# One-hot rows of the expert weights: two tokens taking turns in memory instead of four

## The chip, the cores and the metric

The kernel runs on one core of one Trainium2 chip. The metric is the device time of one execution in microseconds; the median of 3 runs of the kernel before is 2192.8 us (2192.29 to 2193.07). All arithmetic is in the kernel.

## The reference

The program is a model of two blocks over 256 tokens with 1024 features: two layers of attention of three kinds between feed-forwards, then a block with two recurrent mixers (mLSTM and gated linear attention, with a context of 256 tokens), and at its end a layer of 16384 small experts (128 x 128 of them), whose part matters here:

- Eight heads give every token scores against 128 first and 128 second keys; the 16 best of a head's sums name 16 experts by (first index, second index), with a softmax over the 16 as weights. So a token has 8 x 16 = 128 pairs.
- An expert is a row u and a row v of 1024 numbers. The output is the sum over a token's 128 pairs of weight x gelu(x . u[expert]) x v[expert]. Here gelu is the activation function.

## The kernel before, in words

Features or pairs lie on the 128 partitions, tokens along the free dimension. All large products take each operand in two float32 parts (`mm3`, lines 256 to 258: three matmuls of 128 x 128 stationary by 256 moving columns). Weights come by DMA in pieces of 128 x 1024, and are split into their two parts by ScalarE (line 218, `wH`) and VectorE (line 219, `wL`); each of these has three buffers.

The expert layer (`peer`) does not gather experts. It computes the activation of all 16384 experts for all tokens into A [128, 128 tiles, 256 tokens] (`u_chunk`, two tiles each, 64 chunks), multiplies A by a matrix G that holds a token's weight where one of its pairs falls and 0 elsewhere, and then takes the product with all rows v (`v_chunk`, 64 chunks). The first 32 chunks of u run while pairs are chosen. The other 32 run between the steps that make G: 16 groups of 16 tokens, a group being four calls of `g_unit` (four tokens each) and two chunks.

`g_unit` makes G for four tokens. The 128 pairs of a token lie on the partitions. In a tile `o` of f16 it makes, for each pair, the row of 128 that is 1 at the second index (part 0), the row that is 1 at the first index (part 1), and the latter times the pair's weight in two parts (2 and 3):

- line 1268, VectorE: compares a table of indices `i4` with the tokens' indices `ix`; parts 0 and 1, 1024 elements per partition.
- line 1270, VectorE: part 2 = part 1 x the weights' high part `wH` (512 elements).
- line 1272, ScalarE: part 3 = part 1 x the weights' low part `wL`, one copy of 128 elements per token.
- line 1275, TensorE: for each token two matmuls in f16 add up part 2 or 3 (stationary) times part 0 (moving) over the 128 pairs: a tile of G, 128 first by 128 second indices, in PSUM.
- lines 1278 and 1280: VectorE multiplies the first n1 tiles of A by it, ScalarE stores the rest for later. n1 grows from 64 to 124 over the groups.

In `o` the four tokens are the innermost dimension: element i of a row is followed by element i of the next token's row. So a row that a matmul reads has its elements four apart, 8 bytes; the same goes for ScalarE's copies. `o` has two buffers, PSUM's bank `at` four. The order on each engine is laid down when the program is built; in the trace, all but the first matmuls of line 1275 stand in runs of 16, two calls of `g_unit`, with the 48 matmuls of half a group's chunks (one chunk) between two runs.

Of the kernel before, what the change touches and what calls it, by code (L numbers as in the profile page):

```python
# [29 lines left out]

def tiles_of(w, cols):
    """[K, N] -> [128, len(cols), K/128, 128]: column tiles as stationary operands; -1 pads with 0."""
    w = np.asarray(w)
    kt = w.shape[0] // 128
    w = np.concatenate([w, np.zeros((w.shape[0], 1), w.dtype)], axis=1).reshape(kt, 128, -1)
    return w[:, :, np.asarray(cols)].transpose(1, 2, 0, 3)
# [6 lines left out]
def rows_of(w):  # L43
    """[K, N] -> [128, K/128, N]."""
    w = np.asarray(w)
    return w.reshape(-1, 128, w.shape[1]).transpose(1, 0, 2)


def col_of(v):
    """[..., n*128] -> [128, n]: a vector over features, one column per tile."""  # L50
    return np.asarray(v).reshape(-1, 128).T
# [96 lines left out]
def gate_rows(mg, glr):  # L148
    """Rows of the tile of gates: quadrants ig d0 + glr d0, ig d1 + glr d1, f d0, f d1."""
    g = [-1] * 128  # L150
    for d in range(2):
        for h in range(4):
            g[32 * d + h] = mg + 8 * d + h
            g[64 + 32 * d + h] = mg + 8 * d + 4 + h
        if glr is not None:
            for r in range(16):
                g[32 * d + 16 + r] = glr + 16 * d + r
    return g
# [46 lines left out]
class W:  # L205
    """Weights [128, cols] of DRAM in two float32r parts, in pieces of cut columns."""
# [22 lines left out]
class Halves:  # L229
    """A [128, KT, T] array in two tiles, indexed [:, k] or [:, a:b] within one of them."""  # L230
# [11 lines left out]
class K:  # L242
# [5 lines left out]
    # -- streams of weights --------------------------------------------------------------------  # L248
# [3 lines left out]
    def mm3(self, out, w, c, x, k, first, last, skip=False):  # L252
        """out += W[:, c:c+128]^T x[k], each operand in two parts."""
# [6 lines left out]
    def mm3t(self, out, x, k, t, w, c, n, first, last, pick=lambda v: v):  # L260
        """out[tok, n] += x[k][:, tok tile t]^T W[c:c+n]."""
# [10 lines left out]
    # -- norms -----------------------------------------------------------------------------------  # L272
# [14 lines left out]
    def stats_many(self, items):  # L287
        """For each x [128, kt, T]: 1 / rms, over all partitions [128, T], and per token [128, 2]."""
# [17 lines left out]
        out = []  # L306
# [12 lines left out]
    def sums(self, x, g=None, sq=None):  # L319
        """Sums of the squares of x [128, KT, T] (times g[k]) over the features: PSUM [128 tokens, 2].  # L320
        sq [128, KT, T]: where the squares go, otherwise to tiles of their own."""
# [21 lines left out]
    def spread(self, r, tag, pool):  # L343
        """r [128 tokens, 2] -> [128, T], the same on every partition."""
# [8 lines left out]
    def split_scaled(self, x, g, kt, tag="x"):  # L353
        """The two parts of x[k] * g[k]."""
# [16 lines left out]
    def hold(self, t):  # L371
        """The load of t that follows waits for the tile of the feed-forward that is under way: weights come first."""
        if self.mark is not None:
            self.nc.gpsimd.tensor_copy(t[:, :1], self.mark[:, :1])
# [8 lines left out]
    # -- feed-forward ----------------------------------------------------------------------------  # L383
    def ffn(self, name, l, side=iter(()), every=1, down=1):
        """side: steps of something else, taken between tiles."""
# [34 lines left out]
    # -- attentions ------------------------------------------------------------------------------  # L420
    def rope(self, dst, src, n, tab, rows=slice(0, 128), split=None):
        """dst = rope(src); src, dst [rows, n, T]; halves of a head lie in one tile."""
# [17 lines left out]
    def head(self, q, k, bias, scale, v, o):  # L440
        """One head: q, k [rows, T] features first; bias [128, 384]; v(kt) [128 keys, 64]; o PSUM [64, T]."""
# [28 lines left out]
    def mixer(self, l):  # L470
# [17 lines left out]
        # indexer  # L488
# [30 lines left out]
        # scores of the indexer  # L519
# [42 lines left out]
        # queries and keys of C  # L562
# [28 lines left out]
        # top 64 of each row: eight at a time are taken out  # L591
# [12 lines left out]
        def attend(h, q, k, bias, scale, v):  # L604
            """Head h of the 16; its half of a tile of features, which is split when both halves are there."""
# [39 lines left out]
        # output: the tiles of B and C first, then those of A  # L645
# [14 lines left out]
    # ==== second block =========================================================================  # L660
    def modulation(self, pool):
        """Steps that make mod[:, j, 0/1]: tile j of the 6 D values for the latents / the context."""
# [21 lines left out]
    def first_norm(self):  # L684
        """x of the first block, and its modulated norm in two parts."""
# [11 lines left out]
        # the second norm's mean square is that of x * gain times r1^2  # L697
# [12 lines left out]
    def modnorm(self, x, g, sc, sh, tag="x"):  # L710
        """rmsnorm(x) * g * (1 + sc) + sh in two parts."""
# [8 lines left out]
    def split_mod(self, x, a, rb, sh, tag="x"):  # L720
        """The two parts of x[k] * a[k] * rb + sh[k]."""
# [20 lines left out]
    def conv(self, dst, p, j, rows):  # L742
        """dst [128, T] = conv(p), p in PSUM, channels of tile j."""
# [8 lines left out]
    def values(self, n, xs, dst):  # L752
        """dst(t) [128 tokens, 512]: values, tokens on partitions, in steps."""
# [12 lines left out]
    def projections(self, xs, lat, gk, gq, mk, mq, mv):  # L766
        """All projections but the gates, in steps; mk, mq before their silu."""
# [8 lines left out]
        def keys(c, lo, n):  # L776
            """Tiles lo.. of src[c]; the first ones may be gq[1]."""
# [22 lines left out]
    def side(self, xs, lat):  # L800
        """Projections of one side, and what the states of both mixers need of it, in steps."""
# [5 lines left out]
        # gates, rows 32 d + h; logarithms of the sigmoids of the gates and of the decay of the GLA  # L807
# [20 lines left out]
        # tiles that the states of the mLSTM need lie outside of the pool: those of the context are made late  # L828
# [9 lines left out]
        # running sums and maxima of the mLSTM  # L838
# [17 lines left out]
        # the running maximum: m[j], M[j] = max(m[j], ce[j]), m[j+1] = be[j] + M[j]  # L856
# [17 lines left out]
        # sums of the decay of the GLA  # L874
# [10 lines left out]
        # exponentials of the mLSTM  # L885
# [5 lines left out]
        # a[j] = exp(m[j] - M[j]) on every partition  # L891
# [24 lines left out]
        # per token columns  # L916
# [6 lines left out]
        # exponentials of the GLA  # L923
# [17 lines left out]
        if lat:  # L941
# [4 lines left out]
            # weights of the pairs of tokens of the mLSTM, before the products of queries and keys  # L946
# [20 lines left out]
        # states of the GLA  # L967
# [47 lines left out]
        # keys of the mLSTM, tokens on partitions  # L1015
# [7 lines left out]
        # states of the mLSTM: C[:, h, d] = [e, (d, n)]  # L1023
# [20 lines left out]
    def gates(self, xs, gr, mo):  # L1044
        """Output gates, in steps: tiles 0-3 of the GLA, tiles 4-7 of the mLSTM; tile i lies in src[6 + (i + 1) // 2]."""
# [12 lines left out]
    def norm_heads(self, h, dst, g, gate):  # L1058
        """dst(t-major h [128, 2, 4, 128]) -> parts of gate * g * h / rms(h), features first."""
# [22 lines left out]
    def mlstm_out(self, s, gates):  # L1082
# [26 lines left out]
        # 1 / max(|den|, exp(-m))  # L1109
# [51 lines left out]
    def top16(self, z, vals, idx, n):  # L1161
        """The 16 largest of each row of z [128, n], in order, and where they stand; z is used up."""
# [8 lines left out]
    def peer(self):  # L1171
# [5 lines left out]
        with ExitStack() as es:  # L1177
            op = es.enter_context(tc.tile_pool(name="po", bufs=1))
            # activations of the experts, tile j: those of second index j; its end is scratch at first
            A = op.tile([128, 128, T], F32, name="A")  # L1180
            # per pair of a token, four tokens at a time: second indices, first indices; weights times 2^14 in two parts
# [3 lines left out]
            i4 = op.tile([128, 128, 4], F16, name="i4")  # L1185
            nc.vector.tensor_copy(i4, iota[:, :, None].to_broadcast([128, 128, 4]))
# [3 lines left out]
            def u_chunk(c, g=None):  # L1190
                """Two tiles of experts. While G is made for the tokens of group g, what falls on them waits in y,
                which is returned with its place; before (None) all of it is kept, after (4) all of it is weighted."""
# [22 lines left out]
            with tc.tile_pool(name="route", bufs=1) as kp:  # L1215
# [27 lines left out]
                # softmax over the chosen  # L1243
# [19 lines left out]
            def g_unit(u, n1):  # L1263
                """The weights of the experts for four tokens: times what the first n1 tiles hold, stored for the rest."""
                q = self.bank("at")
                o = op2.tile([128, 4, 128, 4], F16, name="o", tag="tmp", bufs=2)
                t = slice(4 * u, 4 * u + 4)
                v.tensor_tensor(o[:, :2], i4[:, None].to_broadcast([128, 2, 128, 4]),  # L1268
                                ix[:, u, :, None, :].to_broadcast([128, 2, 128, 4]), op=OP.is_equal)
                v.tensor_tensor(o[:, 2], o[:, 1], wH[:, None, t].to_broadcast([128, 128, 4]), op=OP.mult)  # L1270
                for i in range(4):
                    nc.scalar.activation(o[:, 3, :, i], o[:, 1, :, i], AF.Copy, scale=wL[:, 4 * u + i:4 * u + i + 1])  # L1272
                for i in range(4):
                    for n in range(2):
                        nc.tensor.matmul(q[:, 128 * i:128 * i + 128], o[:, 2 + n, :, i], o[:, 0, :, i],  # L1275
                                         start=n == 0, stop=n == 1)
# [41 lines left out]
            # x comes back to where the weights were  # L1318
# [16 lines left out]
    def choose(self, kp, s, best, ij, rank):  # L1335
        """s [128, 2, 128]: scores by both halves -> the 16 best pairs: their sums, ij [128, 2, 16]: both indices.
        rank [128, 16, 16]: the second dimension's index."""
# [9 lines left out]
        # a pair of ranks (r1, r2) has (r1 + 1) (r2 + 1) - 1 pairs before it, none smaller: all 16 of r2 for the first  # L1347
        # r1 and 8 for each of the others are enough
# [24 lines left out]
    def context(self):  # L1373
        """What the second block takes from the context, in steps."""
# [149 lines left out]
```

## Time and profile before

| | |
|---|---|
| median of 3 runs | 2192.8 us (2192.29 to 2193.07) |
| profiled execution, first to last instruction (span) | 2190.6 us |
| TensorE busy | 2130.0 us, 97% |
| VectorE busy | 1583.2 us, 72% |
| ScalarE busy | 1172.2 us, 54% |
| mean granted TensorE clock | 0.991 of full speed |

The profile holds one execution. Its time is known as the span alone, from the first instruction to the last; what lies around the span isn't recorded, and the median stands 2.2 us above it. PE is TensorE, PEld its loads of stationary operands, DVE VectorE, ACT ScalarE, SP the queue that issues DMAs. A record of a matmul lasts until its result is out, so records overlap, and the distance between two starts tells what one costs. In rows in order of time, like instructions that follow one another stand as one row with their count, and idle time ahead of a row stands behind it in brackets, with what ended it.

### The profile page before, as it was taken

To read this page: it belongs to the slowest core of one execution; us is meant where nothing else is said; L and a number is where in the kernel's file an instruction comes from. 1 tells how busy PE (TensorE), PEld (TensorE's weight loads), DVE (VectorE), ACT (ScalarE), POOL (GpSimd) and SP (SyncE) were. 2 spreads that over 40 slices of the span, in tenths; PEclk is the share of its full clock that TensorE was granted. 3 is DMA by queue.
4 is the path that set the end of the run, shared out by engine and by line. 5 is a ranking of instruction groups with operands and counts; after the bars stand their busy time and mean duration, and the time that the engine had idled before them with its cause. 6 is when DMAs were issued, how large, how long until landed. Compare 5 with 4: busy or idle time off the path is not lost. (4 is left out here: it accounts for less than half of the span.)

```text
span 2190.6 us, 43018 instructions
## 1 busy us (share of the span) xinstructions
PE 2130.0 (97%) x17204; PEld 2050.1 (94%) x17204; DVE 1583.2 (72%) x3195; ACT 1172.2 (54%) x2003; POOL 8.0 (0%) x15
## 2 busy tenths in 40 slices
PE   8999999999999999998998998999999999999998
PEld 8999879998999997998997888999999999999997
DVE  6766967786787796777658768888877775555555
ACT  5544465444444445556446545454687775444444
POOL 0000000000000000000000000000000000000000
PEclk9999999999999999999999999999999999999999
DMA  6666435666787752454563434555544445555553
GB/s 225 220 201 188 149 96 172 205 214 227 251 271 238 224 161 87 156 190 163 160 201 112 142 99 159 182 187 182 168 136 143 141 138 180 190 188 188 190 187 125
DMA packets 115112, 385.35 MB, mean 176 GB/s; under 512 B 12768, under 2 KB 13920, under 8 KB 114784
## 3 DMA queue, kind: packets, MB, share of 16 engines
q1 hardware_dynamic: 114912, 382.61, 54.1%
q8 instruction: 135, 2.21, 0.4%
q14 instruction: 65, 0.53, 0.1%
HBM read 380.46 MB, written 2.10 MB: 175 GB/s over the span
## 5 line engine op out<-in xcount | busy, mean ns | idle before, releaser
L219 DVE TENSOR_TENSOR wL<-raw,wH 128x1024 fp32r<-128x1024 f32 (+3 forms) x716 | 812.4, 1138 | 352.0 <-ACT wH L218 349.6
L218 ACT ACTIVATE wH<-raw 128x1024 fp32r<-128x1024 f32 (+3 forms) x716 | 707.9, 992 | 635.4 <-PE mm L257 443.8
L256 PE MATMUL mm<-xH,wH 128*128 128x256 f32 x2952 | 839.8, 285 | 11.1 <-ACT xH L360 7.2
L258 PE MATMUL mm<-xH,wL 128*128 128x256 f32 x2952 | 836.4, 284 | 9.2 <-DVE wL L219 9.0
L257 PE MATMUL mm<-xL,wH 128*128 128x256 f32 x2952 | 835.6, 283 | 0.7 <-DVE xL L1080 0.4
L256 PEld LDWEIGHTS mm<-xH,wH 128*128 128x128 f32 x2952 | 560.4, 190 | 15.8 <-ACT xH L360 7.5
L258 PEld LDWEIGHTS mm<-xH,wL 128*128 128x128 f32 x2952 | 559.9, 190 | 15.5 <-DVE wL L219 12.1
L257 PEld LDWEIGHTS mm<-xL,wH 128*128 128x128 f32 x2952 | 560.0, 190 | 4.1 <-issue 1.7
L257 PE MATMUL mm<-hl,wH 128*128 128x256 f32 x1024 | 285.8, 279 | 0.0
L256 PE MATMUL mm<-hl,wH 128*128 128x256 f32 x1024 | 285.8, 279 | 0.0
L258 PE MATMUL mm<-hl,wL 128*128 128x256 f32 x1024 | 285.8, 279 | 0.0
L258 PE MATMUL mm<-hH,wL 128*128 128x256 f32 x704 | 197.7, 281 | 8.9 <-DVE wL L219 8.8
L256 PE MATMUL mm<-hH,wH 128*128 128x256 f32 x704 | 196.3, 279 | 0.0
L257 PE MATMUL mm<-hL,wH 128*128 128x256 f32 x704 | 196.3, 279 | 0.0
L256 PEld LDWEIGHTS mm<-hl,wH 128*128 128x128 f32 x1024 | 192.4, 188 | 0.0
L257 PEld LDWEIGHTS mm<-hl,wH 128*128 128x128 f32 x1024 | 192.4, 188 | 0.0
L258 PEld LDWEIGHTS mm<-hl,wL 128*128 128x128 f32 x1024 | 192.4, 188 | 0.0
L258 PEld LDWEIGHTS mm<-hH,wL 128*128 128x128 f32 x704 | 132.1, 188 | 11.7 <-DVE wL L219 11.7
L676 DVE SCALAR_TENSOR_TENSOR prod<-raw,cv 128x1024 f32<-128x1024 f32 x64 | 78.3, 1224 | 75.8 <-DMA raw<-wmod 75.0
L256 PEld LDWEIGHTS mm<-hH,wH 128*128 128x128 f32 x704 | 132.1, 188 | 0.0
L257 PEld LDWEIGHTS mm<-hL,wH 128*128 128x128 f32 x704 | 132.0, 188 | 0.0
L1272 ACT ACTIVATE o<-o,gL 128x128 f16<-128x128 f16 x256 | 96.2, 569 | 13.3 <-DVE o L1268 10.4
(451 smaller groups left out, 2514.4 us busy)
## 6 DMA issues: line engine op xcount, KB each, us to landing
raw<-ffn_gu SPq DMA_DIRECT2D x174, 512.0 KB, 4.7
raw<-ut SPq DMA_DIRECT2D x128, 512.0 KB, 3.9
raw<-vt SPq DMA_DIRECT2D x128, 512.0 KB, 3.8
raw<-win SPq DMA_DIRECT2D x58, 512.0 KB, 4.4
raw<-wmod SPq DMA_DIRECT2D x48, 512.0 KB, 4.6
raw<-ffn_d SPq DMA_DIRECT2D x64, 384.0 KB, 3.2
raw<-ffn_d SPq DMA_DIRECT2D x64, 320.0 KB, 3.4
raw<-wout SPq DMA_DIRECT2D x24, 512.0 KB, 3.7
```

What stands on the lines that cost most here:

```text
L218: k.nc.scalar.activation(H[:, :n], raw[:, :n], AF.Copy)
L219: k.nc.vector.tensor_tensor(L[:, :n], raw[:, :n], H[:, :n].bitcast(F32), op=OP.subtract)
L256: mm(out, H, xH[:, k], start=first, stop=False, skip_group_check=skip)
L257: mm(out, H, xL[:, k], start=False, stop=False, skip_group_check=skip)
L258: mm(out, L, xH[:, k], start=False, stop=last, skip_group_check=skip)
L676: nc.vector.scalar_tensor_tensor(out, raw, 1.0, cv[:, D * i:D * i + D], op0=OP.mult, op1=OP.mult, accum_out=self.mod[:, j, i:i + 1])
L1272: nc.scalar.activation(o[:, 3, :, i], o[:, 1, :, i], AF.Copy, scale=wL[:, 4 * u + i:4 * u + i + 1])
```

## The change

Tokens take turns in pairs. `o` becomes [parts, 2 pairs of tokens, 128, 2 tokens], so that a row's elements lie two apart, 4 bytes. The table of indices has two copies of each index instead of four (`i2`, 256 elements instead of 512). The comparison and the weighting still take 1024 and 512 elements in one instruction each; their repeated operand (`ix`, `wH`) is now read in runs of two tokens, each repeated 128 times, instead of runs of four. The copies and the matmuls have the same counts and sizes. The rest of the edit takes out comments, which moves lines: 1268, 1270, 1272 and 1275 become 1269, 1272, 1275 and 1279.

```diff
-            i4 = op.tile([128, 128, 4], F16, name="i4")
-            nc.vector.tensor_copy(i4, iota[:, :, None].to_broadcast([128, 128, 4]))
+            i2 = op.tile([128, 128, 2], F16, name="i2")
+            nc.vector.tensor_copy(i2, iota[:, :, None].to_broadcast([128, 128, 2]))
...
             def g_unit(u, n1):
                 q = self.bank("at")
-                o = op2.tile([128, 4, 128, 4], F16, name="o", tag="tmp", bufs=2)
+                o = op2.tile([128, 4, 2, 128, 2], F16, name="o", tag="tmp", bufs=2)
                 t = slice(4 * u, 4 * u + 4)
-                v.tensor_tensor(o[:, :2], i4[:, None].to_broadcast([128, 2, 128, 4]),
-                                ix[:, u, :, None, :].to_broadcast([128, 2, 128, 4]), op=OP.is_equal)
-                v.tensor_tensor(o[:, 2], o[:, 1], wH[:, None, t].to_broadcast([128, 128, 4]), op=OP.mult)
+                v.tensor_tensor(o[:, :2].rearrange("p n b i t -> p (n b) i t"), i2[:, None].to_broadcast([128, 4, 128, 2]),
+                                ix[:, u].rearrange("p n (b t) -> p (n b) t", t=2)[:, :, None, :]
+                                .to_broadcast([128, 4, 128, 2]), op=OP.is_equal)
+                v.tensor_tensor(o[:, 2], o[:, 1], wH[:, t].rearrange("p (b t) -> p b t", t=2)[:, :, None, :]
+                                .to_broadcast([128, 2, 128, 2]), op=OP.mult)
                 for i in range(4):
-                    nc.scalar.activation(o[:, 3, :, i], o[:, 1, :, i], AF.Copy, scale=wL[:, 4 * u + i:4 * u + i + 1])
+                    nc.scalar.activation(o[:, 3, i // 2, :, i % 2], o[:, 1, i // 2, :, i % 2], AF.Copy,
+                                         scale=wL[:, 4 * u + i:4 * u + i + 1])
                 for i in range(4):
                     for n in range(2):
-                        nc.tensor.matmul(q[:, 128 * i:128 * i + 128], o[:, 2 + n, :, i], o[:, 0, :, i],
-                                         start=n == 0, stop=n == 1)
+                        nc.tensor.matmul(q[:, 128 * i:128 * i + 128], o[:, 2 + n, i // 2, :, i % 2],
+                                         o[:, 0, i // 2, :, i % 2], start=n == 0, stop=n == 1)
                 g = q.rearrange("p (t j) -> p j t", j=128)
```

Instruction by instruction, every engine has the same list in the same order before and after; the one thing that differs is the cast that fills the table of indices, 128x512 before and 128x256 after.

## Rows read from the trace of the kernel before

**Rows 1.** The page: busy time (share) xinstructions; the shares of the chain by line.

```profile
PE 2130.0 (97%) x17204; PEld 2050.1 (94%) x17204; DVE 1583.2 (72%) x3195; ACT 1172.2 (54%) x2003; POOL 8.0 (0%) x15
...
PE mm L256 11%; PE mm L257 11%; PE mm L258 11%; PE at L1275 3%; PE at L256 1%; PE at L257 1%; PE at L258 1%; DVE wL L219 0%; PE at L1235 0%; PE mm L1151 0%; PE mm L1156 0%; PE mm L1103 0%; PE at L339 0%; PE at L1138 0%; ACT wH L218 0%
```

**Rows 2.** Stretch: its us, PE, PEld, DVE, ACT, POOL busy (xcount), clock, DMA share, GB/s.

```profile
1577.00:1814.00 237.00, 236.36 (x1995) 233.30 (x1995) 178.71 (x314) 184.51 (x473) 0.00 (x0) 1.00 0.43 142
```

**Rows 3.** List of waits, 1577 to 1814 us: total, times, longest.

```profile
DVE A L1278 <- PE at L1275: 24.4, 28, 1.6
DVE wL L219 <- ACT wH L218: 23.1, 24, 1.9
...
PE at L1275 <- DVE o L1270: 0.6, 1, 0.6
```

**Rows 4.** Line 1275: weight loads and matmuls, shortest/median/longest record in ns.

```profile
L1275 PEld LDWEIGHTS <-o x512: 111/117/138, 1578.8 to 1812.8; 128*128 128x128 f16 x171
L1275 PE MATMUL at<-o x512: 272/298/301, 1578.8 to 1812.9; 128*128 128x128 f16 x171
```

**Rows 5.** TensorE in order of time: start us, length us, work (two places).

```profile
1689.86 2.07 PE L1275 MATMUL at<-o 128*128 128x128 f16 x16
...
1691.88 0.28 PE L257 MATMUL mm<-xL,wH 128*128 128x256 f32 x1
...
1697.32 0.28 PE L258 MATMUL mm<-xH,wL 128*128 128x256 f32 x1
1697.44 2.06 PE L1275 MATMUL at<-o 128*128 128x128 f16 x16
...
1795.96 2.06 PE L1275 MATMUL at<-o 128*128 128x128 f16 x16
```

**Rows 6.** TensorE in order of time, float32 matmuls with 328 columns.

```profile
214.61 0.31 PE L265 MATMUL mm<-wH,xH 128*128 128x328 f32 x1
...
216.55 0.31 PE L266 MATMUL mm<-wL,xH 128*128 128x328 f32 x1
```

**Rows 7.** Weight loads in order of time, a pair at the start of the stretch.

```profile
1579.48 0.15 PEld L1275 LDWEIGHTS <-o 128*128 128x128 f16 x2
```

**Rows 8.** VectorE in order of time: one round, and a late group of two.

```profile
1693.86 1.22 DVE L219 TENSOR_TENSOR wL<-raw,wH 128x1024 fp32r<-128x1024 f32 x1
1695.00 0.42 DVE L1270 TENSOR_TENSOR o<-o,gH 128x512 f16<-128x512 f16 x1
...
1797.11 0.66 DVE L1278 TENSOR_TENSOR A<-A,at 128x480 f32<-128x480 f32 x1 [1.56 <-PE at L1275]
1798.05 0.66 DVE L1278 TENSOR_TENSOR A<-A,at 128x480 f32<-128x480 f32 x1 [0.29 <-PE at L1275]
...
1803.63 1.23 DVE L219 TENSOR_TENSOR wL<-raw,wH 128x1024 fp32r<-128x1024 f32 x1 [1.27 <-ACT wH L218]
```

**Rows 9.** VectorE by line: shortest/median/longest in ns, first and last start.

```profile
L400 DVE TENSOR_TENSOR gu<-mm,rb x88: 654/687/693, 23.6 to 1085.2; 128x512 f32<-128x512 f32 x88
...
L486 DVE TENSOR_TENSOR ak<-mm,rb x6: 414/415/415, 262.8 to 873.7; 128x256 f32<-128x256 f32 x6
...
L1250 DVE TENSOR_TENSOR gt<-gt,sm x1: 415/415/415, 1573.6 to 1573.6; 128x256 f32<-128x256 f32 x1
...
L1268 DVE TENSOR_TENSOR o<-i,ix x64: 683/686/694, 1577.3 to 1807.5; 128x1024 f16<-128x1024 f16 x64
...
L1270 DVE TENSOR_TENSOR o<-o,gH x64: 414/419/426, 1578.2 to 1809.2; 128x512 f16<-128x512 f16 x64
```

**Rows 10.** ScalarE: line 1272; copies side by side (L456); two places in time.

```profile
L1272 ACT ACTIVATE o<-o,gL x256: 530/567/597, 1578.4 to 1810.2; 128x128 f16<-128x128 f16 x128
...
L456 ACT ACTIVATE e<-z,nm 128x128 f32<-128x128 f32 x32 | 12.6, 394 | 5.9 <-DVE nm L452 5.9
...
1595.01 2.71 ACT L1272 ACTIVATE o<-o,gL 128x128 f16<-128x128 f16 x8 [0.29 <-DVE o L1268]
...
1794.16 1.48 ACT L1272 ACTIVATE o<-o,gL 128x128 f16<-128x128 f16 x4
```

## The prediction

> **What bounds the kernel now.** I read the page first, then the sums by stretch, the two lines that make the weights of the experts, and last the order of time inside one round. TensorE is busy for 97% of the span [rows 1], so the question of any change is whether it shortens TensorE's own work or only something beside it. The chain that ended last is made of matmuls, and one entry of it is the matmul of line 1275, with 3% of the span, some 66 us [rows 1]. That is the line that the change re-lays. All of it lies between 1577 and 1814 us, where TensorE is busy 236.4 of 237.0 us while VectorE is busy 178.7 and ScalarE 184.5, at a granted clock of 1.00, the level of 2.4 GHz [rows 2]. The list of waits in the same stretch says the same from the other side: VectorE waits for TensorE (24.4 us) and for ScalarE (23.1), and TensorE waits for VectorE 0.6 us in all [rows 3].
>
> A busy share does not say what a matmul costs here, since the records overlap: each of the 512 matmuls on line 1275 has a record of 298 ns [rows 4], yet sixteen of them together take 2.07 us [rows 5]. The distance from start to start is what counts: (2.07 - 0.298) / 15 = 0.118 us. There are 30 such runs of 16 in the trace, one every 7.58 us (1689.86 to 1697.44), and 16 short runs with the other 32 matmuls at the stretch's start. Between two runs stand 48 float32 matmuls with 256 columns; from 1691.88 to 1697.32 they make 46 steps of 0.118 us [rows 5]. So a matmul of 128 columns in f16 costs exactly what one of 256 columns costs. That is the odd number on which all rests.
>
> **The change part by part.** *The moving operand.* Before, the 128 columns of one token lie 8 bytes apart; afterwards 4 bytes. The float32 operands lie 4 bytes apart, and they run at 0.118 us for 256 columns [rows 5] and (216.55 - 214.61) / 13 = 0.149 us for 328 [rows 6]. The slope is 31 ns / 72 columns = 0.43 ns per column, with about 8 ns on top; 128 columns at that rate are 118 - 128 x 0.43 = 63 ns. The matmul of line 1275 needs 118, as if every column took two steps. I take it that the wide step causes this, and that at 4 bytes these matmuls run like the float32 ones, at 63 ns. Bounds: half of 118 is 59 ns if nothing of the 8 ns stays; 118 ns if the step is not the cause. I take 63, since the float32 rows are the nearest in step and clock.
>
> *The weight loads.* Each of these matmuls has its own load. Could the load be the limit? Its records last 111 to 138 ns [rows 4], but two loads issued together take 0.15 us in all [rows 7], so the second ends 0.03 to 0.04 us after the first: a load passes in about that time and the rest is latency. It also goes on beside the matmul before it (the second load of that pair starts before the first matmul has streamed). So a load can be hidden behind 63 ns. If it can't, the pitch is 63 + 33 = 96 ns.
>
> *Sum on TensorE.* Of a run of 16, 15 steps shrink; the last step stays, since it ends with the load of a float32 weight. 30 runs x 15 x (118 - 63) ns = 24.8 us. The 16 short runs are cut up by waits for ScalarE's copies, and I count their inner steps (0.9 us at most) as nothing.
>
> *Is the cover there?* After the change a round lasts 7.58 - 0.83 = 6.75 us, and the others must keep up. For the run at 1697.44, the last weighting by VectorE ends at 1695.42 [rows 8], 2.0 us ahead. The smallest lead in the 30 runs is late: ScalarE's last copy ends at 1795.64 [rows 10] and the second half of that run, which reads it, starts at 1795.96 + 8 x 0.118 = 1796.90 [rows 5], 1.2 us later. These copies come after that of a weight, whose buffer TensorE frees in the middle of its 48 float32 matmuls, so the lead moves along with the runs; only 8 x 55 ns = 0.44 us of it goes for the second half. Late in the stretch, where the products on line 1278 are longest, VectorE still idles 1.56 + 0.29 + 1.27 = 3.1 us in a group of two rounds (15.2 us) [rows 8]; the group loses 1.7 us, so 1.4 us of idle time are left. Part of that idling is waiting for TensorE, which ends with the shorter run. So I expect the cover to hold to the end; if it fails in the late half alone, it takes back about 1 us in each of eight groups, 8 us in all.
>
> *VectorE's two operations.* Comparing 1024 elements takes 686 ns and weighting 512 takes 419 ns [rows 9]. On float32 256 elements take 415 ns, 512 take 687 and 1024 take 1.22 us [rows 8, 9], some 1.06 ns for each more; the two f16 operations take what half as many float32 elements take, so they go two elements at a time. The count of elements is the same afterwards, but the repeated operand comes in runs of two tokens instead of four: 4 bytes read again and again. No row shows such runs in f16. From below: nothing changes. From above: the pair is lost, (1.22 - 0.686) + (0.687 - 0.419) = 0.80 us for each of 64 units, 51 us in all. I take nothing, because in float32 an operand that repeats one 4-byte word 16 times runs at full speed: line 1250 takes 415 ns for 256 elements, line 486 with plain operands 414 [rows 9]. The Trainium skill, "Vector Engine (DVE) Microarchitecture Reference", section on measured stream behaviour, says that a port keeps its rate only with runs of two or more neighbouring 4-byte words, and gives 1.73 against 1.05 ns per column for one source that hops every element. An estimate by that page, for 1536 elements in 768 pairs: 64 x 768 x 0.68 ns = 33 us more on VectorE, 212 in all, just what TensorE needs afterwards; line 1250 speaks against it, at least for a word that is repeated in place.
>
> *ScalarE's copies.* 256 copies of 128 elements take 567 ns each, 304 ns apart in a run of eight ((2.71 - 0.57) / 7 = 0.306); 128 float32 elements side by side with a pointer operand take 394 ns [rows 10]. So the wide step costs latency here too, and I expect about 400 ns afterwards. TensorE doesn't wait for it outside the short runs; worth nothing on the path.
>
> *The table of indices* is half as large. It is filled once, ahead of the stretch, while TensorE has other work, and I count nothing for it.
>
> The order of the instructions on every engine is as before, so no wait is added. Sum: the profiled span of 2190.6 us becomes 2190.6 - 24.8 = 2165.8. The median of the runs is 2.2 us above that span, and I carry this over: 2168 us.
>
> **The rivals.** *No gain.* The 118 ns have another cause (stream and load of f16 take turns: 63 + 55), and the step doesn't matter. For it: no f16 matmul with a narrow step is in the trace to compare. Against it: 118 is so exactly two steps per column, and ScalarE's copies with the same step are slow too. Time: 2192.7. The Trainium skill, "Advanced Engine Details and Errata", section on SBUF cachelines, says that two hits on a line of 16 bytes are enough for full speed; a step of 8 bytes has two, so by that rule nothing is gained and this rival holds. The 118 ns at that step against 63 for the same bytes per column side by side speak against it, unless the load is the cause.
>
> *Half a gain.* The loads come into view: 96 ns per matmul, 450 x 22 ns = 9.9 us, time 2183; or less of them, 80 ns, 17.1 us, time 2176. For it: the load records don't get shorter than 111 ns. Against it: the pair of loads. The Trainium skill, "TensorE: Matmul & The Clock Gate", section on the back-to-back issue gap, gives about 81 ns for a stream of loads and matmuls with 128 columns; 118 - 81 = 37 ns by 450 would be 16.7 us.
>
> *Slower: VectorE loses its pair.* Both operations go one element at a time. VectorE's 178.7 us [rows 2] become 230.1, or 14.4 us for each of 16 groups, over the 13.3 us that TensorE would need; from 13.3 on VectorE sets the pace. Without any wait the stretch takes 230 us (2186); with the waits for ScalarE's copies, 23.1 us [rows 3], left as they are, 253 (2209). Those copies are made only when TensorE frees a buffer, so I put it at 2203. Against it: only the inner run changes, and it is still a run.
>
> **How the numbers follow.** Forecast 0.66, from 2165 (59 ns instead of 63 and the short runs' inner steps) to 2176 (cover lost late); half a gain 0.14; no gain 0.12; VectorE slower 0.08. The range goes from 2161, 4 us below the forecast's best for the short runs, which go in the rhythm of ScalarE's copies and whose waits I can't split, to 2185, which takes in half a gain: 0.8 together. A measurement of this kernel can tell about 0.2%, 4.4 us, from no change: faster is forecast and half a gain, 0.80; same is no gain, 0.12; slower 0.08.
>
> **What would show it.** Runs of 16 on line 1275 should take 1.2 to 1.3 us instead of 2.07, one every 6.7 to 6.8 us; the stretch should end near 1789 instead of 1814; the comparison and weighting should stay at 686 and 419 ns, the copies fall to about 400. TensorE's waits for VectorE should stay below 2 us. I am wrong if the run stays at 2 us (step not the cause), if it is 1.5 to 1.75 (loads), if either VectorE operation nears its float32 time, or if the runs shrink and the round does not: then the wait for the one-hot rows has become the bound.

## The result, and the profile after

The kernel after takes 2160.97 us (median of 4 runs, 2160.77 to 2166.35) against 2192.94 us before in the same set; the ratio of their runs is 0.9861, with a 95% interval of 0.9849 to 0.9873. That is 32 us less, between 27.9 and 33.1. The prediction was 2168, faster by 25, with a range from 2161 to 2185: the median stands at the range's lower edge, 0.03 us under it, and a later set of the same kernel (e6 below, 2163.67) stands inside.

The profiled execution has a span of 2159.1 us. On its page TensorE is as full as before (97%), but the entry of the f16 matmul in the chain, now on line 1279, has fallen from 3% [rows 1] to 1%.

```profile
PE 2100.6 (97%) x17204; PEld 2022.3 (94%) x17204; DVE 1580.4 (73%) x3195; ACT 1159.6 (54%) x2003; POOL 8.0 (0%) x15
...
PE mm L256 12%; PE mm L257 11%; PE mm L258 11%; PE at L1279 1%; PE at L256 1%; PE at L257 1%; PE at L258 1%; DVE wL L219 0%; PE at L1236 0%; PE mm L1151 0%; PE mm L1156 0%; PE mm L1103 0%; PE at L339 0%; PE at L1138 0%; ACT wH L218 0%
```

In order of time on TensorE, a run of 16 now takes 1.09 us, where it took 2.07 [rows 5], and the next one starts 6.67 us later instead of 7.58:

```profile
1687.48 1.09 PE L1279 MATMUL at<-o 128*128 128x128 f16 x16
...
1694.15 1.09 PE L1279 MATMUL at<-o 128*128 128x128 f16 x16
```

From start to start that is (1.09 - 0.218) / 15 = 58 ns on the mean. The median step is 57 ns, but the first step of a run takes 71. Over the 30 runs the mean fell from 117.8 to 58.2 ns, so 15 steps make 0.89 us. The step from a run's last matmul to the next float32 one fell from 46 to 27 ns and adds 0.02. That is the whole of the 0.91 us by which a round became shorter, and nothing was given back.

The lines that make and use the one-hot rows, weight loads and matmuls first, then the comparison, the weighting and ScalarE's copies (shortest/median/longest in ns, first and last start in us):

```profile
L1279 PEld LDWEIGHTS <-o x512: 96/97/103, 1576.0 to 1781.6; 128*128 128x128 f16 x171
L1279 PE MATMUL at<-o x512: 218/218/234, 1576.0 to 1781.7; 128*128 128x128 f16 x171
...
L1269 DVE TENSOR_TENSOR o<-i,ix x64: 672/684/693, 1574.5 to 1778.0; 128x1024 f16<-128x1024 f16 x64
...
L1272 DVE TENSOR_TENSOR o<-o,gH x64: 403/416/428, 1575.4 to 1779.8; 128x512 f16<-128x512 f16 x64
...
L1275 ACT ACTIVATE o<-o,gL x256: 419/431/467, 1575.6 to 1779.9; 128x128 f16<-128x128 f16 x128
```

VectorE's two operations are unchanged (686 and 419 before [rows 9]); the copies fell from 567 [rows 10] to 431 ns. From the first to the last f16 matmul the stretch takes 1781.7 - 1576.0 = 205.7 us, where it took 1812.9 - 1578.8 = 234.1 [rows 4]: 28.4 us less. In the stretch TensorE is still the engine without idle time (first row), and its only wait for VectorE is the one that it had before [rows 3]:

```profile
1576.00:1781.70 205.70, 205.70 (x1976) 203.72 (x1977) 173.65 (x308) 170.31 (x467) 0.00 (x0) 1.00 0.48 157
```

```profile
DVE A L1282 <- PE at L1279: 9.0, 17, 0.7
```

```profile
PE at L1279 <- DVE o L1272: 0.6, 1, 0.6
```

The columns of the first row are those of [rows 2], of the others those of [rows 3]. What shrank most is VectorE's waiting for these matmuls at the product with A, from 24.4 to 9.0 us.

The two spans differ by 31.5 us, 3 us more than the stretch. The first f16 matmul started 2.8 us earlier than before, after the same work but for the cast of the table. A later profile of the same kernel (e6 below) shows that it belongs to the execution, not to the change: there the same kernel started it at 1578.5.

### The profile page after: what moved, and what is told of

It is laid out like the page before. It is cut to its first block, busy times and chain, and to the rows that moved or that the text cites. A ratio compares the mean times of both kernels' runs of the same rounds, so it can differ in the third digit from the quotient of the medians.

```text
span 2159.1 us, 43018 instructions
## 1 busy us (share of the span) xinstructions
PE 2100.6 (97%) x17204; PEld 2022.3 (94%) x17204; DVE 1580.4 (73%) x3195; ACT 1159.6 (54%) x2003; POOL 8.0 (0%) x15
## 5 line engine op out<-in xcount | busy, mean ns | idle before, releaser
L1275 ACT ACTIVATE o<-o,gL 128x128 f16<-128x128 f16 x256 | 85.9, 436 | 9.9 <-DVE o L1269 7.1
```

Of the source, the lines that this page charges most:

```text
L1275: nc.scalar.activation(o[:, 3, i // 2, :, i % 2], o[:, 1, i // 2, :, i % 2], AF.Copy, scale=wL[:, 4 * u + i:4 * u + i + 1])
```

## The experiments

In e1 to e5 and e8 to e10 the kernel before is kept, and only the elements that the f16 matmuls read are changed: `f` is the tile `o` as one row of 2048 f16, so that any distance can be read without a change to VectorE's or ScalarE's work. What is read belongs to other tokens, and the weights of the experts are not the reference's. The numbers are taken from start to start within a run of 16 (a step; the median over the 15 steps of 30 runs, and where it says so the mean, which the longer first step of a run raises), and from the first to the last f16 matmul (the stretch, 234.1 us before and 205.7 after). The edits are shown without the line that makes `f` and without what stays.

**e1, the moving operand alone.**

```diff
-nc.tensor.matmul(q[:, 128 * i:128 * i + 128], o[:, 2 + n, :, i], o[:, 0, :, i],
+nc.tensor.matmul(q[:, 128 * i:128 * i + 128], o[:, 2 + n, :, i], f[:, i:i + 256:2],
```

> The kernel before, four tokens taking turns, with one thing changed: the moving operand of the f16 matmuls reads 128 elements that lie 4 bytes apart instead of 8 (elements of two tokens, so the weights of the experts are not the reference's; everything else is computed as before). The stationary operand keeps 8 bytes, ScalarE's copies too. Theory A (the moving operand's step costs): start to start falls from 118 to 57 or 58 ns as in the kernel after, a run of 16 from 2.07 to about 1.1 us, time 2161 to 2167. Theory B (the load of the stationary operand at 8 bytes is the limit): 118 ns stay, time 2193. Theory C (the loads at 8 bytes come into view once the stream is short): 75 to 100 ns, time 2173 to 2185.

Measured: 2165.69 us against 2192.28 before in its set, ratio 0.988 (0.986 to 0.9901). A run of 16 takes 1.15 or 1.16 us. The median step is 60 ns; the first step of a run takes 89 ns (71 in the kernel after), so that the mean is 62.4. The stretch takes 208.1 us.

```profile
1690.13 1.15 PE L1276 MATMUL at<-o 128*128 128x128 f16 x16
```

The moving operand alone gives 26 of the stretch's 28.4 us. Theory A holds; C, with 75 to 100 ns, is not there. Loads that still read 8 bytes apart cost 2.5 ns per matmul on the mean (62.4 against 59.9 in e5 below, where they read 4 apart), half of it in the first step of a run.

**e2, the stationary operand alone.**

```diff
-nc.tensor.matmul(q[:, 128 * i:128 * i + 128], o[:, 2 + n, :, i], o[:, 0, :, i],
+nc.tensor.matmul(q[:, 128 * i:128 * i + 128], f[:, 512 * (2 + n) + i:512 * (2 + n) + i + 256:2], o[:, 0, :, i],
```

> The kernel before with the stationary operands of the f16 matmuls read 4 bytes apart and the moving one still 8 (again elements of two tokens, so the weights of the experts are not the reference's). Theory A: 118 ns stay, time 2193 within 0.2%; at most the loads' records get shorter (from 117 to 97 ns as in the kernel after). Theory B: 57 ns, time about 2161. Theory C: 118 ns here too, since the stream is the longer of the two.

Measured: 2189.5 us against 2192.28, ratio 0.9984 (0.9967 to 1.0001), so no difference can be told. 117 ns from start to start, the stretch 233.1 us. The loads' records stayed at 117 ns too (median).

```profile
1693.88 2.03 PE L1276 MATMUL at<-o 128*128 128x128 f16 x16
```

The load at 8 bytes was not the limit. Theory B falls, and with it the form of *no gain* in which stream and load take turns.

**e5, both operands,** with the other engines left on four tokens: the two edits above together.

> The kernel before with both operands of the f16 matmuls read 4 bytes apart (elements of two tokens, not the reference's weights), while VectorE and ScalarE work on four tokens taking turns as before. The kernel after minus this one is what the layout does for VectorE's two operations and ScalarE's copies. Theory A, with the other engines off the path: the time of the kernel after, 2161, within 2 us; copies stay at 567 ns. Rival: the shorter copies (431 ns after) carry part of the gain: 3 to 8 us above the kernel after.

Measured: 2160.98 us against 2193.97 in its set, ratio 0.9871 (0.9841 to 0.9901); 59 ns, the stretch 206.5 us, copies 569 ns. So the shorter copies of the kernel after and its other way of repeating operands are worth at most 0.8 us in the stretch. The mean step alone, 59.9 against 58.2 ns, makes 0.77 of that, so the copies carry nothing that can be told. Where the 1.7 ns come from is open: the rows here start 0, 2, 4 or 6 bytes into their part of the tile, after it is 0 or 2 into a block, but the steps don't follow that order (a matmul with a row at 6 bytes takes 58 ns on the mean, one at 4 bytes 61).

**e6, the kernel after once more.**

> The kernel after once more, for a second profile and more times. The first profile was 31.5 us shorter than that of before, of which 27.5 us lie between the first and the last f16 matmul and 4 us outside, 2.8 ahead of it and 1.1 behind. If the 4 us outside are chance, this profile differs there by some us from the first; if they belong to the change, the first f16 matmul starts near 1576.0 us again and the time is 2161 again.

Measured: 2163.67 us (2163.07 to 2165.8) against 2193.97, ratio 0.9872 (0.985 to 0.9894).

```profile
L1279 PE MATMUL at<-o x512: 218/218/234, 1578.5 to 1784.2; 128*128 128x128 f16 x171
```

The stretch takes 205.7 us again, but begins at 1578.5, where the kernel before began it at 1578.8 [rows 4]. The expectation's split of the 31.5 us (27.5, 2.8 and 1.1) was off: by the rows it is 28.4 in the stretch, 2.8 ahead of it and 0.3 behind. Over all twelve profiles, with the same work ahead of it but for the cast of the table, the first f16 matmul starts between 1574.0 (e5) and 1583.3 us (e2), with no order in it. So of the 31.5 us between the first two profiles about 3 are chance; the change is worth 28 to 29 us. The later set, 30.3 us between the medians, agrees within its interval.

**e4, e8, e3 and e9: the distance.** The moving operand is read 2, 12, 16 and 32 bytes apart (only this argument of the matmul is shown):

```diff
+f[:, 128 * i:128 * i + 128]      # e4, 2 bytes
+f[:, i:i + 768:6]                # e8, 12 bytes
+f[:, i:i + 1024:8]               # e3, 16 bytes
+f[:, i:i + 2032 + 1:16]          # e9, 32 bytes
```

> The kernel before with the moving operand read side by side, 2 bytes apart (not the reference's weights), the stationary operand at 8 bytes. If the 57 ns of the kernel after are the stream of 128 columns at full speed, nothing is left to gain from a narrower step: the same 57 ns and the same time as with 4 bytes (2161 to 2167). If 4 bytes still cost something: below 57 ns, 2 to 5 us less than with 4 bytes.

> The kernel before with the moving operand read 16 bytes apart (every eighth element of the two one-hot parts, not the reference's weights). It asks for the unit of the cost. If every element outside a run of neighbouring 4-byte words costs one more step, whatever the distance, 118 ns stay and the time is 2193. If it is lines of 16 bytes of which a step of 8 uses two elements, one element per line costs more: 170 to 225 ns, 450 x 55 to 105 ns = 25 to 47 us on top, time 2218 to 2240.

> The kernel before with the moving operand read 12 bytes apart (not the reference's weights). Steps of 2 and 4 bytes gave 56 to 60 ns from start to start, 8 gave 118, 16 gave 230. Theory P (the cost is proportional to the distance, one step of the stream for each 4 bytes passed over): 174 ns. Theory L (lines: a whole line is fetched and one of 16 bytes serves as many columns as lie in it): 12 bytes leave 1.33 columns in a line, 230 / 1.33 = 173 ns as well. Theory Q (powers of two: anything above 8 pays like 16): 230 ns.

> The same with 32 bytes, where the theories part. Theory P: 8 steps per column, about 455 ns, 450 x 225 = 100 us above the kernel with 16 bytes, about 2375 us. Theory L: one column per line at 16 as at 32 bytes, 230 ns, 2275 us. Theory Q: not told, 230 or more.

| kernel | bytes apart | step in ns, median (mean) | stretch, us | time, us (before in its set) |
|---|---|---|---|---|
| e4 | 2 | 56 (58) | 206.0 | 2163.19 (2192.28) |
| e1, e5, after | 4 | 60 (62), 59 (60), 57 (58) | 208.1, 206.5, 205.7 | 2165.69, 2160.98, 2160.97 |
| before | 8 | 118 (118) | 234.1 | 2192.94 |
| e8 | 12 | 175 (174) | 262.7 | 2222.61, one run (2191.17) |
| e3 | 16 | 230 (230) | 315.8 | 2274.81 (2192.28) |
| e9 | 32 | 233 (233) | 315.2 | 2272.58, one run (2191.17) |

Ratios: e4 0.9867 (0.9844 to 0.9889), e3 1.037 (1.0346 to 1.0395). A run of 16 in e8, e3 and e9, one row of each kernel:

```profile
1696.55 2.96 PE L1276 MATMUL at<-o 128*128 128x128 f16 x16
```

```profile
1707.57 3.84 PE L1276 MATMUL at<-o 128*128 128x128 f16 x16
```

```profile
1693.98 3.90 PE L1276 MATMUL at<-o 128*128 128x128 f16 x16
```

Elements side by side (e4) gain nothing over the kernel after. Against e1, whose loads also read 8 bytes apart, they gain 2.1 us in the stretch: there the step of 4 bytes still costs a little. 32 bytes cost hardly more than 16: theory P falls and theory L holds. 12 bytes give 175 where L has 173, and Q would have 230. The stream behaves as if it fetched a line of 16 bytes in about 1.8 ns (233 / 128), and needed four columns out of each to run at the 56 ns of columns side by side. Two columns in a line, as before the change, make 118. That the unit is a line of 16 bytes is inferred from these six distances; nothing in the trace names it. e8 and e9 are one run each, and their part here is the step, not the time.

e3 missed its expectation, 170 to 225 ns and 25 to 47 us: the stretch grew by 81.7 us, of which the longer steps explain 450 x 112 ns = 50. Most of the rest is the clock, which the expectation had left out: the steps between float32 matmuls add up to 200 us in this stretch and to 171 before, 29 us. Right after some runs of 16 the float32 matmuls go 0.21 us apart instead of 0.118, and the granted clock of that piece is 0.50, the level of 1.2 GHz; a little later in the same round it is 1.00 again (columns as in [rows 2] and [rows 5]):

```profile
1701.10 0.41 PE L258 MATMUL mm<-xH,wL 128*128 128x256 f32 x1
1701.32 0.41 PE L256 MATMUL mm<-xH,wH 128*128 128x256 f32 x1
```

```profile
1700.60:1703.10 2.50, 2.50 (x14) 2.50 (x13) 2.19 (x7) 2.01 (x7) 0.00 (x0) 0.50 0.00 0
1703.40:1707.50 4.10, 4.10 (x37) 4.10 (x35) 2.44 (x3) 1.75 (x3) 0.00 (x0) 1.00 0.35 123
```

TensorE shows no gap before it fell: the run's records follow one another without idle time. In the whole stretch the granted clock was 0.50 in 19 pieces, 64.8 us together. With 12 bytes the clock stayed at 1.00 over 1590 to 1840 us.

**e10, loads at 16 bytes.**

```diff
+nc.tensor.matmul(q[:, 128 * i:128 * i + 128], f[:, 1024 + i:1024 + i + 1017:8], f[:, i:i + 256:2],
```

> The kernel before with the moving operand at 4 bytes and the stationary one at 16 bytes (not the reference's weights). With loads at 8 bytes it took 60 ns from start to start, with loads at 4 bytes 59. If loads pay for their step as the stream does but hide behind it as long as they are shorter (32 columns at a time in four parts, so about a quarter of the stream's price): still about 60 ns, at most 75. If loads pay in full at 16 bytes: 100 ns and more, 2180 us and more.

Measured, one run: 2171.09 us (before 2191.17); 64 ns from start to start (67.6 on the mean, the first step of a run 118), the stretch 211.0 us. The loads do pay for their distance, since with the moving operand at 4 bytes their median record grows from 98 ns (e5, 4 bytes) to 113 (e1, 8) and 146 (16). But most of it stays hidden, 7.7 ns per matmul above e5 on the mean:

```profile
L1276 PEld LDWEIGHTS <-o x512: 141/146/173, 1579.8 to 1790.7; 128*128 128x128 f16 x171
```

**e7, no turns: the rival with VectorE.**

```diff
-i4 = op.tile([128, 128, 4], F16, name="i4")
+i1 = op.tile([128, 128], F16, name="i1")
...
-o = op2.tile([128, 4, 128, 4], F16, name="o", tag="tmp", bufs=2)
+o = op2.tile([128, 4, 4, 128], F16, name="o", tag="tmp", bufs=2)
...
-ix[:, u, :, None, :].to_broadcast([128, 2, 128, 4]), op=OP.is_equal)
-v.tensor_tensor(o[:, 2], o[:, 1], wH[:, None, t].to_broadcast([128, 128, 4]), op=OP.mult)
+ix[:, u].rearrange("p n t -> p (n t)")[:, :, None].to_broadcast([128, 8, 128]), op=OP.is_equal)
+v.tensor_tensor(o[:, 2], o[:, 1], wH[:, t, None].to_broadcast([128, 4, 128]), op=OP.mult)
...
```

> No turns at all: each token's rows lie side by side (2 bytes apart), all that the reference asks for is computed. TensorE's runs should be as short as after (57 ns). But the operand that VectorE repeats is now a single element of 2 bytes. Rival of the prediction (VectorE loses its pair): the comparison takes 1.22 instead of 0.69 us and the weighting 0.69 instead of 0.42, 51 us more VectorE work, VectorE sets the pace and the time is 2186 to 2209, as the prediction priced it. If a single repeated element keeps the pair: 686 and 419 ns and the time of the kernel after, 2161.

The copies and matmuls then read `o[:, 3, i]`, `o[:, 1, i]`, `o[:, 2 + n, i]` and `o[:, 0, i]` (cut above).

Measured: 2178.08 us against 2193.97, ratio 0.9926 (0.9902 to 0.995): faster than before, and 14.4 us slower than the kernel after in the same set (2163.67). Within a run the matmuls go 56 ns apart (median), but VectorE has lost its pair, at the upper bounds that the prediction gave (1.22 and 0.687 us), and is hardly ever idle, while TensorE has gaps:

```profile
L1268 DVE TENSOR_TENSOR o<-i,ix x64: 1210/1217/1237, 1578.1 to 1796.0; 128x1024 f16<-128x1024 f16 x64
...
L1270 DVE TENSOR_TENSOR o<-o,gH x64: 676/682/701, 1579.6 to 1797.8; 128x512 f16<-128x512 f16 x64
```

```profile
1580.40:1799.40 219.00, 216.68 (x1971) 204.17 (x1971) 218.43 (x306) 169.61 (x468) 0.00 (x0) 1.00 0.43 146
```

So two tokens are the fewest that keep the pair, and the most that put four columns into a line. The rival's price was too high, and the time lies under the 2186 to 2209 expected: the stretch takes 219.0 us, not 230 to 253. VectorE's waits for ScalarE, 23.1 us before [rows 3], are gone from its list (0.2 us of waiting in all, for TensorE). And the records of operations that follow without a pause overlap: VectorE's in the stretch add up to 242 us, of which 218 are distinct time.

## Why the prediction was right, point by point

- *TensorE bounds the stretch, and the f16 matmul costs two steps per column because its moving operand is read 8 bytes apart:* shown by e1 and e2, one operand at a time; by the distances, two steps is what two columns in 16 bytes cost.
- *At 4 bytes it costs 63 ns, by the line through the float32 matmuls.* This is the term that was mis-sized: 58.2 ns on the mean. Of the 8 ns that I carried over from the float32 matmuls on top of their columns, 3 stay; no run asks why the rest goes. The lower bound (59, half of 118) was the better reading. With 117.8 ns before, 450 x 59.6 = 26.8 us instead of 24.8. The last step of a run, which I let stay, fell by 19 ns, 0.6 us in 30 runs. So a run came out at 1.09 us and a round at 6.67, a little under what I had named as signs (1.2 to 1.3, and 6.7 to 6.8).
- *The short runs at the start count nothing:* they gave 1.05 us, more than the 0.9 that I had allowed at most (the first full run started 12.53 us after the first matmul before, 11.48 after). Together that is 28.4. What the median has beyond that, 3 to 4 us, is put down to the executions, as e6 and the spread of starts suggest: that it stands at the range's edge is half luck of the set, not a term of the sum.
- *The cover is there:* shown by the rounds, which shrink by all that the runs do. Late in the stretch VectorE has 0.31 + 1.13 us of idle time left in a group of two rounds, where I had worked out 1.4:

```profile
1768.15 1.22 DVE L1282 TENSOR_TENSOR A<-A,at 128x480 f32<-128x480 f32 x2 [0.31 <-PE at L1279]
...
1774.14 1.23 DVE L219 TENSOR_TENSOR wL<-raw,wH 128x1024 fp32r<-128x1024 f32 x1 [1.13 <-ACT wH L218]
```

- *Loads hide behind a shorter stream:* shown to 2.5 ns at 8 bytes (e1) and to 7.7 at 16 (e10), both against e5. The rival *half a gain*, and with it the 81 ns of the Trainium skill, "TensorE: Matmul & The Clock Gate", section on the back-to-back issue gap, do not appear here: 57 to 60 ns (median) with one load for each matmul of 128 columns (after, e1, e5).
- *VectorE keeps its pair:* 684 and 416 ns. The rule that I set against it, from the Trainium skill's "Vector Engine (DVE) Microarchitecture Reference", section on measured stream behaviour, would have made them longer; here a word of two f16 that is repeated in place costs no more than a run of four did.
- *No gain, by two hits on a line of 16 bytes:* the rule of the Trainium skill, "Advanced Engine Details and Errata", section on SBUF cachelines, gives a unit that fits the distances, but for TensorE's moving operand in f16 two hits on a line are not enough: they cost 118 ns, and only four came down to 57.
- *ScalarE's copies fall to about 400 ns and don't matter:* 431 ns, and e5 shows that they don't, to 0.8 us.

## What to carry to other kernels

Measure a matmul from start to start and compare it with one of known width: 128 columns at the price of 256 were the sign that the moving operand's elements lie too far apart. Lay an f16 moving operand so that four columns fall into 16 bytes, even where several tiles take turns in memory; a stationary operand may lie wider, since behind 128 columns most of its load hides. Where the same rows are made by VectorE from a repeated 16-bit operand, keep at least two elements innermost in it.

## What the runs showed of the hardware that I had not expected

The price of the moving operand's distance stops at 16 bytes (230 ns at 16, 233 at 32). And the clock can fall though TensorE shows no idle time: in e3 the granted clock fell to 0.50 behind runs of matmuls read 16 bytes apart, and over the stretch of e9 (32 bytes) it averaged 0.90, while at 12 bytes it stayed at 1.00. The distance, and with it the elements read, is all that differs between these kernels; by what it brings the clock down is not shown.

ScalarE pays for distance on short copies, in its record and hardly in its pace: 128 elements take 387 ns side by side (e7), 431 at 4 bytes and 567 at 8; from start to start the copies go 306 ns apart at 8 bytes, (2.49 - 0.43) / 7 = 294 at 4 and 293 side by side (medians 306, 294, 293).

```profile
1757.31 2.49 ACT L1275 ACTIVATE o<-o,gL 128x128 f16<-128x128 f16 x8 [1.06 <-DVE o L1269]
```
